# A hybrid encoder layer on one core: branch mix by row block with its weights loaded once, six PSUM banks for the mix, and three projection weight slots ahead of LayerNorm 1

## The chip, the cores and the metric

The kernel runs on one NeuronCore of a Trainium2 chip. A core has a matrix engine (TensorE, PE in the profile), a vector engine (VectorE, DVE), a scalar engine (ScalarE, ACT), GpSimd (POOL) and SyncE (SP), which issues the DMAs here. Each engine works through its own queue in order and waits for the others by semaphores. The metric is the time of one execution in device microseconds; a kernel's time is the median of its runs.

## What is computed

One layer with post-norm residuals, for two request groups (BATCH 1 and DEC_BATCH 1, 512 tokens each, D_MODEL 1024) that share all weights:

```python
x = layernorm(ALPHA * x + 0.5 * swiglu(x, ffn1_wgu, ffn1_wd))          # FFN1, LN1
h = x @ w_in                                                           # MLA, RWKV and gate columns
br_a = mla(h) @ p_mla                                                  # attention branch
br_b = rwkv7(h) @ p_rwkv                                               # recurrent branch, 512 channels
gates = sigmoid(h[..., OFF_GATE:] + b_gate).reshape(b, s, 2, D_MODEL)
mix = (gates[:, :, 0] * br_a + gates[:, :, 1] * br_b) @ w_o            # the branch mix, then w_o
x = layernorm(ALPHA * x + mix)                                         # LN2
x = layernorm(ALPHA * x + cross(x, layernorm(mem)))                    # LN3
x = layernorm(ALPHA * x + 0.5 * swiglu(x, ffn2_wgu, ffn2_wd))          # FFN2, LN4
```

Everything is float32.

## The kernel before

**Layout.** Activations lie with channels on the 128 partitions and the 512 tokens of one group along the row: D_MODEL is eight such tiles (KT), a group one of two (G). Operands are of the type fp32r in the profile: each float32 operand is split into a high and a low part, and a product of a 128 x 128 weight block with a 128 x 512 tile is three matmuls: high by high, high by low, low by high (`Bank.prod`). A `Bank` is one PSUM bank; the ring "a" has four, "b" and "c" two each. `abreast(banks, ws, xs)` computes several rows of an output at once, going over the inner tiles in the outer loop, so that each tile of x serves all rows as soon as it is there. In the profile the parts are called by their tiles: `xh`/`xl` are the high and low parts of x, `yh`/`yl` of the recurrence's output, `mh`/`ml` of the mix, `whl` both parts of a weight slot, `ps` a bank.

**Weights.** Apart from the feed-forward parts, weights come as a stream of 512 KB slots of eight blocks each, in the order of a plan. `Stream.fetch` takes the next one: SP loads it into a raw buffer (`wraw`), ACT casts it to the high part (L246), DVE subtracts to get the low part (L180). There are two raw buffers; the split slots go round rings of buffers (pools `wp` with three and `wide` with one, later `wp` and `wb_pool`). `st.block()` hands out the blocks and fetches the next slot when one is used up.

**Order.** A scheduler sets the order of the instructions on each engine from the order in which the code issues them, its own costs and the dependencies. Two places force it: `Bank` keeps the matmuls of one bank in order, and the DVE engine handed to the kernel (`Held`) puts every instruction issued after `BlockNorm.stats(..., hold=True)` behind the statistics of that layer norm. That includes the subtractions of `Stream.fetch`.

**FFN1 and LN1.** FFN1 multiplies by Strassen's seven products in blocks; its last step, `down_step` for the last entry of DOWN, adds the last sums into x. The sums' products go in a list of eight orders, and before each one `ahead(i)` is called, which fetches weights. LN1 then takes its statistics through transposes on PE (`cc`, `ln_v`, `ln_h` and `x` in PE's L221 rows; `ln_b`, `ln_m`, `rs` on DVE), and a chain on DVE, ACT and POOL normalises and splits x. The first use of x is `compressed`, three rows of w_in (one slot a row) by both groups abreast: 144 matmuls, called c_kv below.

**The recurrence and what runs beside it.** The RWKV recurrence goes head by head (four pairs of heads); each step is a chain of small matmuls (`sn`, `gs`, `uv`) and DVE operations, and matmuls of other parts fill PE's time between them. Its output y is 4 tiles a group; the last tile (the fourth head pair) crosses PE in L216 and L221 rows `ps<-cc,z` (`crossed`) before it can be split to `yh` and `yl`.

**The branch mix.** For group 0 and then group 1, eight rows n: four weight blocks of p_rwkv (half a slot), the gate `gt` and the attention branch `at` by DMA, twelve matmuls into a bank of ring "a", and z = (gt + 1) * sum, z = z + at, split to `mh` and `ml` on ACT and DVE (three DVE operations). The plan lists the four p_rwkv slots twice (`B_MIX` = slots 12 to 16 of stream B), so they are loaded and split once for each group. Of the matmuls, those on the first three tiles of y of the first rows can go before the last head pair is ready: 36 stand ahead of the crossing in PE's order. Then w_o follows, rows 0 to 3 and 4 to 7, each by both groups, one row after the other (`mix_row`), with 24 matmuls a row and its sum added to x for LN2.

Of the kernel before, what the change touches and what calls it, by code (L numbers as in the profile page):

```python
# [22 lines left out]
G = 2  # L23
D = 1024
KT = 8
# [7 lines left out]
ALPHA = 2.0**0.25  # L33
# [25 lines left out]
A_FILL = A_END - 16  # L59

FILL = ((72, 66, 30), (6, 50, 36), (8, 54, 36), (0, 38, 20))
B_MIX = 12, 16
STREAM_B = (
    tiles_of("w_ck", range(4), 8)
    + [("w_cv", k, n) for k in range(8) for n in range(4)]
# [461 lines left out]
            ra, rb = nxt  # L527


def ffn(k, fw, x32, std, rows_of, op_tile, posts, sums, d_h, d_s, norm_of, applied, last=False):  # L530

# [31 lines left out]
    norms, due, going = [], [], []  # L565
# [18 lines left out]
    def down_step(n, u2, u4):  # L584
        m, p0, p1_ = DOWN[n]

        def ahead(i):

            if i == 2 and m == 3:
                while due:  # L590
                    due.pop(0)()
            if i == 2:
                for p in range(p1_, max([p1_, *(b for _, _, b in DOWN[n + 1 : n + 2])])):
                    fetch(p)
# [3 lines left out]

        def add(out, name, u):
            nc.vector.scalar_tensor_tensor(out=out, in0=ps[name].t, scalar=SC, in1=u, op0=ALU.mult, op1=ALU.add)  # L600

        final = n == len(DOWN) - 1

        def more(r, c, u):

# [8 lines left out]
        def summed(i, x):  # L614

            x.add(m // 2)
            if m == 3 and not last:
                if i == 1:  # L620
                    going.append(applied(rows_of[0], norms[0]))
                    for _ in range(3):
                        next(going[0])
                BlockNorm.stats([x], True)
            elif m == 3 and i == 1:
                BlockNorm.stats(norms, True)
# [25 lines left out]
    with posts() as sb:  # L652
# [13 lines left out]
        for g in range(G):  # L666
            xp = [std[g].pair(i) for i in range(KT)]
            banks = [Bank(k, "a") for _ in range(4)]
            ws = [[(o[0][:, i * P : i * P + P], o[1][:, i * P : i * P + P]) for i in range(KT)] for o in w]
            if last:  # L670
                abreast(banks, ws, xp)
            for j in range(2):
                pg, pu = banks[2 * j : 2 * j + 2]
                if not last:
                    for b, o in zip((pg, pu), ws[2 * j : 2 * j + 2]):
                        b.prod(b.t, list(zip(o, xp)))
                s = sb.tile([P, 2, T], F32, name="s", tag="s", bufs=2)[:, 0]
                nc.scalar.activation(out=s, in_=pg.t, func=AF.Silu)
                nc.vector.tensor_tensor(out=s, in0=s, in1=pu.t, op=ALU.mult)
                to_h(s, d_s[j][g], sb)  # L680
            if g == 0:
                for name in ("S1", "S2", "S3"):
                    ops[name] = op_tile(name)
                hold = [(0, slice(0, 2), sb.tile([P, 2, T], F32, name="up", tag="up", bufs=1))]
                for i in range(2):
                    t = sb.tile([P, 1, T], F32, name=("p1", "u4")[i], tag=("p1", "u4")[i], bufs=1)
                    hold.append((2, slice(i, i + 1), t))
                for name, a, b, op in (("S1", "A21", "A22", ALU.add), ("S2", None, "A11", ALU.subtract)):
                    for h in hold:
                        sums_of(name, a, b, op, *h)  # L690
# [7 lines left out]
        for f in range(2 * NP):  # L698
# [41 lines left out]
            if f % 2:  # L740
# [13 lines left out]
                a, b = hs  # L754
# [48 lines left out]
def kernel(  # L803
# [87 lines left out]
    xpools = [x0.enter_context(pool("x0", "right")), rs.enter_context(pool("x1", "right"))]  # L891
    wide = rs.enter_context(pool("ww", "right"))
    plan = [(wa, 0, A_FILL)] + [(wa, A_FILL, A_END)] * G
    plan += [(wb, 0, B_MIX[1]), (wb, *B_MIX), (wb, B_MIX[1], len(STREAM_B) // 8)]
    st = Stream(nc, plan, nc.vector)
    st.use(*[(wp, 3, 2)] * 3, (wide, 1, 0))
    k.ps = ctx.enter_context(pool("banks", space=PSUM))
    with ExitStack() as f1:
# [35 lines left out]

        places = {n: (xpools[0], "x", 4) for n in ("A11", "A12")}
        places.update({n: (xpools[1], "x", 4) for n in ("A22", "S4")}, **{n: (xo, "xo", 6) for n in ("S1", "S2", "S3")})
        ffn(k, fw, x32, xs, (0, 1), op_tiles(places), lambda: pool("post1"), sums1, d_h, d_s, norm1, applied1)

    def gate_out(n, g, h, t):
        nc.scalar.activation(out=t, in_=h, func=AF.Tanh, scale=0.5, bias=hbg[:, n : n + 1])  # L940
# [334 lines left out]
    def acts(kts, name):  # L1275
        return Acts(mixed, "xs", 8, kts, name)

    mix = []
    with pool("mixin", "right") as sm:
        for g in range(G):  # L1280
            mix.append(acts(KT, "m"))
            for n in range(KT):
                w = st.blocks(4)
                gt = sm.tile([P, T], F32, name="gt", tag="gt", bufs=6)
                at = sm.tile([P, T], F32, name="at", tag="at", bufs=6)
                nc.sync.dma_start(out=gt, in_=d_gate[8 + n][:, g])
                nc.sync.dma_start(out=at, in_=d_a[n][:, g])
                b = Bank(k, "a")
                b.prod(b.t, list(zip(w, [ys[g].pair(i) for i in range(4)])))
                z = sm.tile([P, T], F32, name="z", tag="z", bufs=3)  # L1290
                nc.vector.scalar_tensor_tensor(out=z, in0=gt, scalar=1.0, in1=b.t, op0=ALU.add, op1=ALU.mult)
# [30 lines left out]
    norms = norms_of(2)  # L1322
    w = []

    def mix_row(g, n):
        b = Bank(k, "a")
        b.prod(b.t, list(zip(w[n], [mix[g].pair(i) for i in range(KT)])))
        sum_row(norms[g], g, n, b, 0.5 / ALPHA)

    for n0 in (0, 4):  # L1330
        w += [st.blocks(KT) for _ in range(4)]
        for g in range(G):
            for n in range(n0, n0 + 4):
                mix_row(g, n)
            if (n0, g) == (4, 0):
                norms[0].stats()
    x2 = [None, None]
# [115 lines left out]

    places = {n: (mixed, "xs", 8) for n in ("A11", "A12", "A22", "S4")}
    places.update({n: (keep, "xs", 4) for n in ("S1", "S2")}, S3=(of, "xo", 2))
    ffn(k, fw, y32, x3, (1, 0), op_tiles(places), lambda: pool("post2"), sums2, d_h, d_s, norm4, applied4, True)


def softmax(k, sb, s, scale):
# [544 lines left out]
```

## Time and profile before

| | us |
|---|---|
| time, median of 3 runs (lowest to highest) | 2775.86 (2774.26 to 2776.49) |
| the profiled execution | 2775.84 |
| its span, first to last instruction | 2774.1 |
| mean granted PE clock (share of full speed) | 0.963 |
| PE busy / DVE busy | 2605.6 / 2123.8 |
| last transposes of LN1 to the first full run of c_kv matmuls | 684.45 to 700.71 |
| last crossing of the recurrence to the first w_o matmul | 1773.98 to 1822.64 |

A profile's row reads: start and length in microseconds, engine, line of kernel.py, operation, the tile written and the tiles read, the shapes, how many instructions the row gathers, and in brackets how long the engine was idle before it and which engine's result ended that. L216 and L221 are the helper lines through which all matmuls and transposes go, L180 the one for DVE, L246 the cast to the high part, so a row is told by its tiles. PE rows can overlap, since matmuls are pipelined; the distance between starts is what one costs.

### The profile page before, as it was taken

What the parts mean: (1) busy time and instruction counts of PE and PEld (TensorE: products, weight loads), DVE (VectorE), ACT (ScalarE), POOL (GpSimd) and SP (SyncE); (2) the same over time, 40 slices, a digit from 0 to 9 for tenths busy, and PEclk for the clock granted to TensorE, in tenths of its full rate; (3) what the DMA queues carried; (4) which work ended last, traced back from release to release, by engine and by line L of the source; (5) the groups of instructions that cost most, each with busy time, mean ns of one, the idle gap of its engine ahead of it and who ended that gap; (6) DMA issues with size and microseconds to landing.
All of it is one profiled execution on the core that took longest, in us unless ns stands there. A gap on an engine that the chain in (4) does not pass through costs nothing.

```text
span 2774.1 us, 41500 instructions
## 1 busy us (share of the span) xinstructions
PE 2605.6 (94%) x15600; PEld 2079.9 (75%) x15600; DVE 2123.8 (77%) x3749; ACT 1095.9 (40%) x2008; POOL 699.1 (25%) x479
## 2 busy tenths in 40 slices
PE   8999999997899999997989888899999999999996
PEld 7888887785767777776777676677777888887784
DVE  7888887999366777758475768656798888887987
ACT  5334342223353555444443432224554343342222
POOL 0323332443100001133133321103032332332443
PEclk9999999999989999998899898999999999999998
DMA  4344437661244333343434354441101433447751
GB/s 171 130 150 160 152 145 296 235 235 57 95 165 150 112 106 111 111 143 129 131 109 131 119 178 126 161 174 42 54 31 67 161 144 138 152 162 267 273 202 68
DMA packets 164776, 398.18 MB, mean 144 GB/s; under 512 B 41120, under 2 KB 47520, under 8 KB 164576
## 3 DMA queue, kind: packets, MB, share of 16 engines
q1 hardware_dynamic: 164576, 395.53, 40.8%
q8 instruction: 124, 2.03, 0.3%
q14 instruction: 76, 0.62, 0.1%
HBM read 261.50 MB, written 133.96 MB: 143 GB/s over the span
## 4 chain that ended last, share of the span: by engine, by line
PE 76%; DVE 15%; ACT 3%; issue 2%; DMA 2%; POOL 1%; SPq 0%; POOLq 0%; ACTq 0%; DVEq 0%
PE ps L216 73%; PE ps L221 3%; DVE whl L180 2%; DVE dw L180 2%; DVE z L180 1%; DVE x L180 1%; DVE tm L180 1%; DVE rs L180 1%; DVE wt L180 1%; DVE s L180 1%; DVE ln_s L180 1%; DVE phi L180 1%; ACT whl L246 0%; DMA ld<-d_rw 0%; DVE up L180 0%
## 5 line engine op out<-in xcount | busy, mean ns | idle before, releaser
L216 PE MATMUL ps<-xh,whl 128*128 128x512 f32 x2688 | 890.2, 402 | 26.7 <-DVE whl L180 16.8
L216 PE MATMUL ps<-xo,whl 128*128 128x512 f32 x3792 | 899.7, 396 | 14.2 <-DVE z L180 8.5
L216 PEld LDWEIGHTS ps<-xo,whl 128*128 128x128 f32 x3792 | 713.0, 189 | 185.6 <-DVE z L180 6.7
L216 PEld LDWEIGHTS ps<-xh,whl 128*128 128x128 f32 x2688 | 507.8, 190 | 144.2 <-DVE whl L180 20.4
L216 PE MATMUL ps<-xl,whl 128*128 128x512 f32 x1344 | 535.1, 399 | 1.5 <-POOL xl L247 1.5
L180 DVE TENSOR_TENSOR whl<-wraw,whl 128x512 fp32r<-128x512 f32 (+4 forms) x273 | 282.5, 1045 | 63.6 <-ACT whl L246 62.9
L246 ACT CAST whl<-wraw 128x512 fp32r<-128x512 f32 (+4 forms) x318 | 223.9, 715 | 250.1 <-PE ps L216 210.8
L216 PEld LDWEIGHTS ps<-xl,whl 128*128 128x128 f32 x1344 | 255.8, 190 | 55.8 <-POOL xl L247 2.3
L709 POOL TENSOR_TENSOR s<-s,up 128x512 f32<-128x512 f32 x80 | 115.9, 1449 | 626.6 <-DVE up L180 391.1
L246 ACT CAST whl<-wt 128x512 fp32r<-128x512 f32 (+3 forms) x280 | 148.5, 555 | 276.0 <-PE ps L216 164.1
L180 DVE TENSOR_TENSOR whl<-wt,whl 128x512 fp32r<-128x512 f32 (+3 forms) x280 | 216.7, 795 | 10.8 <-ACT whl L246 10.3
L247 POOL TENSOR_TENSOR whl<-wraw,whl 128x1024 fp32r<-128x1024 f32 x45 | 109.1, 2426 | 385.5 <-ACT whl L246 355.4
L246 ACT CAST hop<-s 128x512 fp32r<-128x512 f32 x128 | 79.5, 621 | 238.2 <-POOL s L709 178.0
L180 DVE TENSOR_TENSOR hop<-s,hop 128x512 fp32r<-128x512 f32 x128 | 121.4, 949 | 55.4 <-ACT hop L246 48.0
L180 DVE SCALAR_TENSOR_TENSOR x<-ps,x 128x512 f32<-128x512 f32 x184 | 124.5, 683 | 50.6 <-PE ps L216 50.2
L180 DVE TENSOR_TENSOR wt<-wraw 128x512 f32<-128x512 f32 (+3 forms) x140 | 110.6, 791 | 1.0
L180 DVE TENSOR_TENSOR wt<-wraw,wt 128x512 f32<-128x512 f32 (+3 forms) x140 | 103.1, 737 | 4.2 <-DMA wraw<-in_wf_dram 2.1
L607 POOL TENSOR_TENSOR x<-x,s 128x512 f32<-128x512 f32 x48 | 70.7, 1478 | 129.4 <-DVE x L180 129.4
L247 POOL TENSOR_TENSOR xl<-x,xh 128x512 fp32r<-128x512 f32 x48 | 68.6, 1453 | 91.8 <-ACT xh L246 91.5
L180 DVE TENSOR_TENSOR p<-ps,p 128x512 f32<-128x512 f32 x120 | 82.2, 685 | 7.8 <-PE ps L216 4.8
L607 POOL TENSOR_TENSOR x<-x,z 128x512 f32<-128x512 f32 x48 | 71.3, 1486 | 52.8 <-DVE x L180 49.2
L216 PE MATMUL ps<-mh,whl 128*128 128x512 f32 x256 | 82.2, 401 | 0.0
(328 smaller groups left out, 3728.2 us busy)
## 6 DMA issues: line engine op xcount, KB each, us to landing
d_h<-hop SPq DMA_DIRECT2D x140, 512.0 KB, 2.6
xo<-d_h SPq DMA_DIRECT2D x140, 512.0 KB, 7.2
wraw<-in_wf_dram SPq DMA_DIRECT2D x95, 512.0 KB, 3.4
wraw<-in_wa_dram SPq DMA_DIRECT2D x57, 512.0 KB, 3.5
wraw<-in_wb_dram SPq DMA_DIRECT2D x36, 512.0 KB, 3.4
wraw<-in_wf_dram SPq DMA_DIRECT2D x36, 384.0 KB, 3.9
ld<-d_rw SPq DMA_DIRECT2D x24, 512.0 KB, 4.7
d_gate<-t SPq DMA_DIRECT2D x32, 256.0 KB, 2.4
```

Of the source, the lines that this page charges most:

```text
L180: inst = f(*args, **kw)
L216: self.last = order(k.tc, k.nc.tensor.matmul(out, a, b, start=start, stop=stop), self.last)
L221: self.last = order(self.k.tc, self.k.nc.tensor.transpose(out, a, ident), self.last)
L246: nc.scalar.copy(hi, src)
L247: (low or nc.vector).tensor_tensor(out=lo, in0=src, in1=hi.bitcast(F32), op=ALU.subtract)
L607: eng.tensor_tensor(out=y[r, c], in0=y[r, c], in1=u, op=ALU.add)
L709: nc.gpsimd.tensor_tensor(out=s[:, i], in0=s[:, i], in1=up[:, i], op=ALU.mult)
```

## The change

1. The branch mix goes over rows n outside and groups inside, so each half slot of p_rwkv serves both groups, and the four slots are loaded and split once. The plan no longer lists them twice.
2. The sums of the mix go to six banks, "aaaabb" in turn, instead of four.
3. w_o's first four rows of group 0 go abreast; all other rows as before.
4. The last down step of FFN1 calls `early()` at its fifth product, which fetches the first three slots of w_in. `ffn`'s flag `last` is replaced by the presence of `early`.

```diff
--- before.py
+++ after.py
@@ -59,7 +59,6 @@
 A_FILL = A_END - 16
 
 FILL = ((72, 66, 30), (6, 50, 36), (8, 54, 36), (0, 38, 20))
-B_MIX = 12, 16
 STREAM_B = (
     tiles_of("w_ck", range(4), 8)
     + [("w_cv", k, n) for k in range(8) for n in range(4)]
@@ -527,7 +526,9 @@
             ra, rb = nxt
 
 
-def ffn(k, fw, x32, std, rows_of, op_tile, posts, sums, d_h, d_s, norm_of, applied, last=False):
+def ffn(k, fw, x32, std, rows_of, op_tile, posts, sums, d_h, d_s, norm_of, applied, early=None):
...
@@ -584,11 +585,15 @@
     def down_step(n, u2, u4):
         m, p0, p1_ = DOWN[n]
 
+        final = n == len(DOWN) - 1
+
         def ahead(i):
 
             if i == 2 and m == 3:
                 while due:
                     due.pop(0)()
+            if i == 4 and final and early:
+                early()
             if i == 2:
                 for p in range(p1_, max([p1_, *(b for _, _, b in DOWN[n + 1 : n + 2])])):
                     fetch(p)
@@ -598,8 +603,6 @@
 
         def add(out, name, u):
             nc.vector.scalar_tensor_tensor(out=out, in0=ps[name].t, scalar=SC, in1=u, op0=ALU.mult, op1=ALU.add)
-
-        final = n == len(DOWN) - 1
 
         def more(r, c, u):
 
@@ -616,7 +619,7 @@
 
 
             x.add(m // 2)
-            if m == 3 and not last:
+            if m == 3 and early:
                 if i == 1:
                     going.append(applied(rows_of[0], norms[0]))
                     for _ in range(3):
@@ -667,11 +670,11 @@
             xp = [std[g].pair(i) for i in range(KT)]
             banks = [Bank(k, "a") for _ in range(4)]
             ws = [[(o[0][:, i * P : i * P + P], o[1][:, i * P : i * P + P]) for i in range(KT)] for o in w]
-            if last:
+            if not early:
                 abreast(banks, ws, xp)
             for j in range(2):
                 pg, pu = banks[2 * j : 2 * j + 2]
-                if not last:
+                if early:
                     for b, o in zip((pg, pu), ws[2 * j : 2 * j + 2]):
                         b.prod(b.t, list(zip(o, xp)))
                 s = sb.tile([P, 2, T], F32, name="s", tag="s", bufs=2)[:, 0]
@@ -891,7 +894,7 @@
     xpools = [x0.enter_context(pool("x0", "right")), rs.enter_context(pool("x1", "right"))]
     wide = rs.enter_context(pool("ww", "right"))
     plan = [(wa, 0, A_FILL)] + [(wa, A_FILL, A_END)] * G
-    plan += [(wb, 0, B_MIX[1]), (wb, *B_MIX), (wb, B_MIX[1], len(STREAM_B) // 8)]
+    plan += [(wb, 0, len(STREAM_B) // 8)]
     st = Stream(nc, plan, nc.vector)
     st.use(*[(wp, 3, 2)] * 3, (wide, 1, 0))
     k.ps = ctx.enter_context(pool("banks", space=PSUM))
@@ -934,7 +937,8 @@
 
         places = {n: (xpools[0], "x", 4) for n in ("A11", "A12")}
         places.update({n: (xpools[1], "x", 4) for n in ("A22", "S4")}, **{n: (xo, "xo", 6) for n in ("S1", "S2", "S3")})
-        ffn(k, fw, x32, xs, (0, 1), op_tiles(places), lambda: pool("post1"), sums1, d_h, d_s, norm1, applied1)
+        ffn(k, fw, x32, xs, (0, 1), op_tiles(places), lambda: pool("post1"), sums1, d_h, d_s, norm1, applied1,
+            lambda: [st.fetch() for _ in range(3)])
 
     def gate_out(n, g, h, t):
         nc.scalar.activation(out=t, in_=h, func=AF.Tanh, scale=0.5, bias=hbg[:, n : n + 1])
@@ -1275,17 +1279,17 @@
     def acts(kts, name):
         return Acts(mixed, "xs", 8, kts, name)
 
-    mix = []
+    mix = [acts(KT, "m") for _ in range(G)]
     with pool("mixin", "right") as sm:
-        for g in range(G):
-            mix.append(acts(KT, "m"))
-            for n in range(KT):
-                w = st.blocks(4)
+        for n in range(KT):
+            w = st.blocks(4)
+            for g in range(G):
                 gt = sm.tile([P, T], F32, name="gt", tag="gt", bufs=6)
                 at = sm.tile([P, T], F32, name="at", tag="at", bufs=6)
                 nc.sync.dma_start(out=gt, in_=d_gate[8 + n][:, g])
                 nc.sync.dma_start(out=at, in_=d_a[n][:, g])
-                b = Bank(k, "a")
+
+                b = Bank(k, "aaaabb"[(2 * n + g) % 6])
                 b.prod(b.t, list(zip(w, [ys[g].pair(i) for i in range(4)])))
                 z = sm.tile([P, T], F32, name="z", tag="z", bufs=3)
                 nc.vector.scalar_tensor_tensor(out=z, in0=gt, scalar=1.0, in1=b.t, op0=ALU.add, op1=ALU.mult)
@@ -1322,16 +1326,19 @@
     norms = norms_of(2)
     w = []
 
-    def mix_row(g, n):
-        b = Bank(k, "a")
-        b.prod(b.t, list(zip(w[n], [mix[g].pair(i) for i in range(KT)])))
-        sum_row(norms[g], g, n, b, 0.5 / ALPHA)
+    def mix_rows(g, ns):
+        banks = [Bank(k, "a") for _ in ns]
+        if (g, ns[0]) == (0, 0):
+            abreast(banks, w, [mix[g].pair(i) for i in range(KT)])
+        for n, b in zip(ns, banks):
+            if (g, ns[0]) != (0, 0):
+                b.prod(b.t, list(zip(w[n], [mix[g].pair(i) for i in range(KT)])))
+            sum_row(norms[g], g, n, b, 0.5 / ALPHA)
 
     for n0 in (0, 4):
         w += [st.blocks(KT) for _ in range(4)]
         for g in range(G):
-            for n in range(n0, n0 + 4):
-                mix_row(g, n)
+            mix_rows(g, range(n0, n0 + 4))
             if (n0, g) == (4, 0):
                 norms[0].stats()
     x2 = [None, None]
@@ -1453,7 +1460,7 @@
 
     places = {n: (mixed, "xs", 8) for n in ("A11", "A12", "A22", "S4")}
     places.update({n: (keep, "xs", 4) for n in ("S1", "S2")}, S3=(of, "xo", 2))
-    ffn(k, fw, y32, x3, (1, 0), op_tiles(places), lambda: pool("post2"), sums2, d_h, d_s, norm4, applied4, True)
+    ffn(k, fw, y32, x3, (1, 0), op_tiles(places), lambda: pool("post2"), sums2, d_h, d_s, norm4, applied4)
 
 
 def softmax(k, sb, s, scale):
```

The changed file has one line less ahead of the helpers, so its L179, L215, L220 and L245 are the L180, L216, L221 and L246 of the profile.

DVE at the end of LN1, before: the low parts of the slots (`whl<-wraw,whl`) and the operations of LN1's scaling ahead of them.

```order
L180 TENSOR_TENSOR z<-x_211,ps 128x512
L180 TENSOR_TENSOR s<-s,ps 128x512
L180 TENSOR_TENSOR z<-z,ps 128x512
L180 TENSOR_TENSOR s<-x_211,ps 128x512
L180 TENSOR_TENSOR whl<-wraw,whl 128x1024
L180 TENSOR_TENSOR s<-s,ps 128x512
L180 TENSOR_TENSOR whl<-wraw,whl 128x1024 x3
```

After: among LN1's statistics (`BN_STATS`), the first two slots.

```order
L179 SCALAR_TENSOR_TENSOR z<-ps,z 128x512
L179 BN_STATS ln_b<-ps 128x6 x2
L179 TENSOR_TENSOR whl<-wraw,whl 128x1024
L179 BN_STATS ln_b<-ps 128x6 x3
L179 SCALAR_TENSOR_TENSOR s<-ps,z 128x512
L179 TENSOR_TENSOR whl<-wraw,whl 128x1024
L179 TENSOR_TENSOR x_211<-x_211,s 128x512 x2
L179 SCALAR_TENSOR_TENSOR x_211<-ps,x_211 128x512
L179 BN_STATS ln_b<-ps 128x6 x2
L179 BN_AGGR ln_m<-ln_b 128x2 x2
L179 BN_STATS ln_b<-ps 128x6 x2
L179 BN_AGGR ln_m<-ln_b 128x2 x2
```

The two subtractions moved from the last DVE operations of LN1's scaling to before the first aggregate of its statistics; the third slot's stands some 15 rows further down, between two of FFN1's last sums, and of the x3 before one is left near the end of LN1.

PE at the end of the recurrence, before: `yh_16288` and `yl_16289` are the parts of y of group 0, `cc,z` the crossings of the last head pair.

```order
L216 MATMUL ps<-yl_16289,whl 128x512
L216 MATMUL ps<-yh_16288,whl 128x512
L216 MATMUL ps<-cc,z 64x64 x8
L221 MATMUL ps<-cc,z 64x64 x8
L216 MATMUL ps<-cc,z 64x64 x8
L221 MATMUL ps<-cc,z 64x64 x8
L216 MATMUL ps<-yh_16288,whl 128x512
L216 MATMUL ps<-yl_16289,whl 128x512
L216 MATMUL ps<-yh_16288,whl 128x512 x2
```

After: `yh_16302` and `yl_16303` are those of group 1.

```order
L215 MATMUL ps<-yh_16302,whl 128x512
L215 MATMUL ps<-yl_16303,whl 128x512
L215 MATMUL ps<-yh_16302,whl 128x512 x2
L215 MATMUL ps<-yl_16303,whl 128x512
L215 MATMUL ps<-yh_16302,whl 128x512 x2
L215 MATMUL ps<-yl_16303,whl 128x512
L215 MATMUL ps<-yh_16302,whl 128x512
L215 MATMUL ps<-cc,z 64x64 x8
L220 MATMUL ps<-cc,z 64x64 x8
L215 MATMUL ps<-cc,z 64x64 x8
L220 MATMUL ps<-cc,z 64x64 x8
L215 MATMUL ps<-yh_16288,whl 128x512 x3
```

Ahead of the crossings there now stand matmuls of both groups, 54 instead of 36.

SP in the mix, before: loads of the gate (`gt`), of branch A (`at`) and of weight slots.

```order
L1286 DMA gt<-d_gate_68 128x512
L1287 DMA at<-d_a_130 128x512
L142 DMA wraw<-in_wb_dram 128x1024
L1286 DMA gt<-d_gate_69 128x512
L1287 DMA at<-d_a_131 128x512
L1286 DMA gt<-d_gate_70 128x512
L1287 DMA at<-d_a_132 128x512
L142 DMA wraw<-in_wb_dram 128x1024
L1286 DMA gt<-d_gate_71 128x512
L1287 DMA at<-d_a_133 128x512
```

After: the end of the loads of the mix, and the start of LN2's loads of x.

```order
L1290 DMA at<-d_a_135 128x512
L1289 DMA gt<-d_gate_74 128x512
L1290 DMA at<-d_a_136 128x512
L1289 DMA gt<-d_gate_74 128x512
L1290 DMA at<-d_a_136 128x512
L141 DMA wraw<-in_wb_dram 128x1024 x4
L1317 DMA x_16872<-d_x_0_57 128x1024
L1317 DMA x_16872<-d_x_1_58 128x1024
```

The weight loads that stood between those of the gate and branch A are gone or have moved behind the last of these 32 loads. One slot, w_o's first, moved the other way: its load now stands ahead of all 32.

## The prediction

> **What bounds the kernel now.** I read the page's busy times first, then the chain that ended last, then a table of busy time by stretch, then the rows of the places that the change touches. The page's lines say that TensorE (PE) is the bound almost everywhere: 94% busy, and matmuls carry 76% of the chain.
>
> ```profile
> PE 2605.6 (94%) x15600; PEld 2079.9 (75%) x15600; DVE 2123.8 (77%) x3749; ACT 1095.9 (40%) x2008; POOL 699.1 (25%) x479
> ...
> PE 76%; DVE 15%; ACT 3%; issue 2%; DMA 2%; POOL 1%; SPq 0%; POOLq 0%; ACTq 0%; DVEq 0%
> ```
>
> The change removes no matmul, so it can only pay where PE waits or runs at a low clock. Busy time by stretch (window, length, busy us of each engine with its instructions, the granted PE clock as a share, DMA share, GB/s):
>
> ```profile
> core 0: us, PE busy (x) PEld busy (x) DVE busy (x) ACT busy (x) POOL busy (x), PEclk, DMA share, GB/s
> 640.00:700.00 60.00, 33.91 (x177) 26.45 (x175) 56.93 (x110) 23.37 (x36) 23.89 (x18) 0.84 0.17 67
> 700.00:735.00 35.00, 33.61 (x137) 26.58 (x138) 9.38 (x10) 9.85 (x16) 7.15 (x6) 0.94 0.31 105
> ...
> 1755.00:1780.00 25.00, 18.29 (x204) 14.28 (x204) 18.43 (x51) 4.25 (x9) 3.05 (x3) 0.85 0.42 141
> 1780.00:1823.00 43.00, 40.47 (x158) 32.40 (x159) 34.90 (x52) 15.57 (x23) 0.00 (x0) 0.89 0.58 195
> 1823.00:1920.00 97.00, 96.43 (x419) 77.60 (x418) 54.72 (x81) 30.75 (x44) 21.21 (x15) 0.98 0.26 93
> 2059.00:2092.00 33.00, 29.19 (x112) 22.20 (x111) 32.53 (x52) 19.60 (x30) 18.92 (x12) 0.79 0.20 64
> ```
>
> PE is idle 26 of 60 us at the end of LayerNorm 1 (LN1), while DVE is busy 57 of the 60. Around the branch mix it loses some 9 us and runs at a clock of 0.85 to 0.89. w_o right behind it has no gap. The last row is the start of the second feed-forward part (FFN2), with a clock of 0.79.
>
> **LN1: three weight slots fetched early.** The timeline of PE, then of ACT, DVE, POOL and SP:
>
> ```profile
> 684.45 1.09 PE L221 MATMUL ps<-cc,ln_v 128*128 128x128 f32 x4 [5.70 <-DVE ln_v L180]
> 685.33 1.06 PE L221 MATMUL ps<-cc,ln_h 128*128 128x128 f32 x4
> 700.71 1.22 PE L216 MATMUL ps<-xh,whl 128*128 128x512 f32 x2 [14.32 <-DVE whl L180]
> ```
> ```profile
> 652.82 1.04 ACT L246 CAST whl<-wraw 128x1024 fp32r<-128x1024 f32 x1
> 661.82 1.05 ACT L246 CAST whl<-wraw 128x1024 fp32r<-128x1024 f32 x1 [7.96 <-PE ps L216]
> 674.92 0.81 ACT L359 ACTIVATE x<-z,vc 128x512 f32<-128x512 f32 x1 [12.04 <-DVE z L180]
> ...
> 704.63 1.05 ACT L246 CAST whl<-wraw 128x1024 fp32r<-128x1024 f32 x1 [1.81 <-DMA wraw<-in_wa_dram]
> ...
> 734.52 0.59 ACT L1002 COPY c<-ps 128x512 f32<-128x512 f32 x1 [10.59 <-PE ps L216]
> ```
> ```profile
> 661.78 0.69 DVE L180 SCALAR_TENSOR_TENSOR s<-ps,z 128x512 f32<-128x512 f32 x1 [0.71 <-PE ps L216]
> ...
> 664.52 0.69 DVE L180 SCALAR_TENSOR_TENSOR x<-ps,x 128x512 f32<-128x512 f32 x1 [0.72 <-PE ps L216]
> ...
> 699.37 1.29 DVE L180 TENSOR_TENSOR whl<-wraw,whl 128x1024 fp32r<-128x1024 f32 x1
> ...
> 701.18 1.70 DVE L180 TENSOR_TENSOR whl<-wraw,whl 128x1024 fp32r<-128x1024 f32 x1
> ...
> 705.72 1.88 DVE L180 TENSOR_TENSOR whl<-wraw,whl 128x1024 fp32r<-128x1024 f32 x1 [2.84 <-ACT whl L246]
> ```
> ```profile
> 676.46 1.27 POOL L247 TENSOR_TENSOR xl<-x,xh 128x512 fp32r<-128x512 f32 x1 [23.11 <-ACT xh L246]
> ...
> 688.43 18.08 POOL L247 TENSOR_TENSOR xl<-x,xh 128x512 fp32r<-128x512 f32 x13 [5.72 <-ACT xh L246]
> ```
> ```profile
> 700.68 0.33 SPq L142 DMA_DIRECT2D wraw<-in_wa_dram  x1
> ```
>
> The high halves of the first two slots were made at 652.82 and 661.82, but their low halves only at 699.37 and 701.18, because these subtractions stood behind all of LN1 on DVE. So c_kv (144 matmuls, three rows by two groups, one slot a row) had 4 matmuls done and sent 140 from 700.71. In the changed order the low halves stand among LN1's statistics, two ahead of the first aggregate and one right behind the first spread's numbers, and 18 c_kv matmuls precede LN1's last spread (the x4 and x4 at 684.45).
>
> What it adds: three low halves on DVE within LN1. An undisturbed one takes 1.22 us (1803.01, shown below), so 3.7 us. The two idle gaps at 661.78 and 664.52 take 1.4 of that; the rest, 2.2 us, delays LN1's chain and moves the spread's end from 686.39 to 688.6. On SP the third slot's DMA now stands ahead of the stores of x, and its ACT cast ahead of LN1's scaling: issued when the first raw buffer comes free (about 660), its landing by the old row's 3.95 us (700.68 to 704.63) is 664, before the first scaling at 674.92, so I cost it at nothing. If that cover is gone, ACT holds the scaling, and with it PE.
>
> From 688.6 there are 126 matmuls. Cold ones take 0.44 us and warm ones 0.227 (both worked out below). With 13 cold, as after the stall at 1804.29: 13 x 0.44 + 113 x 0.227 = 31.4, end at 720.0. The same form for before: 700.71 + 13 x 0.44 + 127 x 0.227 = 735.2, against ACT's copy of the second group's first row at 734.52. Gain **15.2**. POOL's low halves of x come every 18.08 / 13 = 1.39 us, and each feeds 9 matmuls (2.05 us), so POOL does not take over.
>
> Bounds: low halves at 1.88 us (705.72, POOL at work) and no early matmul beyond the 4 give 15.2 - 2.0 - 3.2 = 10; no delay of LN1 and a warm clock give 15.2 + 2.2 + 2.8 = 20. I take 15.2, nearest to undisturbed rows, since POOL was idle for 23.11 us before 676.46. [...]
>
> **The mix.** PE's timeline, then the split of one slot on DVE, ACT and SP:
>
> ```profile
> 1744.81 1.14 PE L216 MATMUL ps<-cc,z 64*64 64x64 f32 x16
> ...
> 1748.08 0.97 PE L216 MATMUL ps<-sn,ar 64*64 64x64 f32 x32
> ...
> 1764.76 0.68 PE L216 MATMUL ps<-uv,phi 128*64 128x64 f32 x14
> ...
> 1768.68 0.39 PE L216 MATMUL ps<-yh,whl 128*128 128x512 f32 x1
> 1773.98 1.94 PE L216 MATMUL ps<-cc,z 64*64 64x64 f32 x16 [4.92 <-DVE z L180]
> ...
> 1779.72 0.79 PE L216 MATMUL ps<-yh,whl 128*128 128x512 f32 x1
> ...
> 1783.83 0.62 PE L216 MATMUL ps<-yh,whl 128*128 128x512 f32 x2
> ...
> 1789.27 0.62 PE L216 MATMUL ps<-yh,whl 128*128 128x512 f32 x2
> ...
> 1801.05 0.50 PE L216 MATMUL ps<-yh,whl 128*128 128x512 f32 x1 [0.48 <-ACT whl L246]
> ...
> 1804.29 1.22 PE L216 MATMUL ps<-yh,whl 128*128 128x512 f32 x2 [2.05 <-DVE whl L180]
> ...
> 1810.00 0.75 PE L216 MATMUL ps<-yh,whl 128*128 128x512 f32 x2
> ...
> 1822.64 0.40 PE L216 MATMUL ps<-mh,whl 128*128 128x512 f32 x1
> ```
> ```profile
> 1803.01 1.22 DVE L180 TENSOR_TENSOR whl<-wraw,whl 128x1024 fp32r<-128x1024 f32 x1
> ```
> ```profile
> 1799.95 1.04 ACT L246 CAST whl<-wraw 128x1024 fp32r<-128x1024 f32 x1
> ```
> ```profile
> 1793.28 0.38 SPq L142 DMA_DIRECT2D wraw<-in_wb_dram  x1
> ```
>
> Warm: 24 matmuls from 1783.83 to 1789.27, 0.227 each. Cold: 13 from 1804.29 to 1810.00, 0.44 each. The parts:
> - 18 more matmuls (54 for 36) fit into the 4.92 us before the last crossing, which waits for DVE's z: 18 x 0.227 = 4.1.
> - The crossings took 1773.98 to 1779.72 = 5.74 us cold; the same work between 1744.81 and 1748.08 took 3.27 warm: 2.5.
> - The 11 matmuls from 1779.72 to 1783.83 took 4.11, warm 2.5: 1.6.
> - The second pass over the weights goes, and with it the stalls of 0.48 and 2.05 us (the slot issued at 1793.28 was split at 1799.95 and 1803.01): 2.5; and the cold run behind them, 13 x 0.21 = 2.8. Its four DMAs, four casts and four subtractions were otherwise hidden.
>
> Sum 13.4; w_o could start at 1809.2. DVE was busy 34.9 of the 43 us from 1780 to 1823, which left PE free of it. Without the four subtractions of the second pass (4 x 1.22) it has 30.0 us to do, and PE's share ends in 1809.2 - 1777.3 (the crossings' end, 1773.98 + 3.27) = 31.9. So DVE just keeps up, and is nearly full: whatever it must do more, w_o's first subtractions above all, comes late.
>
> What comes late next is w_o. Its first four rows run abreast and need all four slots soon, where before it needed one. One slot waits loaded but is split only when the last p_rwkv outputs of group 0 leave its memory; the others' DMAs stand on SP behind all 32 loads of gate and branch A. PE's first four or five matmuls need only what is there; then the second slot's low half (some 1.05 of cast and 1.22 of subtraction after the end of the mix, less what overlaps) holds it about 2 us, which DVE's load makes no shorter. A slow clock behind it costs 2.8 or nothing; half is 1.4. Bounds: no wait, 13.4; one whole chain of DMA, cast and subtraction (3.95 + 1.05 + 1.22 = 6.2) plus 2.8 cold leaves 4.4. I take 13.4 - 3.4 = **10.0**, nearer to the end with the shorter chain, since one slot is loaded and two raw buffers take the next.
>
> The row at 1804.29 is cold after an idle time of 2.05 us. [...]
>
> **FFN2's start.** The slots' ring is left in another phase, and the order has one of the first FFN2 splits earlier. The window has 3.8 us of PE idle time and a low clock; between 0 (covered by LayerNorm 3) and 5, I take **1.5**: most of the idle time there waits for FFN2's own splits, but only one of them moves. Everything else keeps its order.
>
> Sum 15.2 + 10.0 + 1.5 = 26.7. The profiled execution took 2775.84 (span 2774.1 and 1.7 around it), practically the median, 2775.86; so 2749.1, say **2749**.
>
> **Rivals.**
> - *w_o starves for a chain* (mix 4.4): total 21.1, 2755. For it speaks SP's order; against, two raw buffers and 15 matmuls for the first two slots ahead of the third.
> - *LN1's chain suffers*: the third cast waits for a buffer or for its DMA on ACT and holds the scaling. LN1 then brings 8 (the wait until the scaling's own cover is gone, 7 us), total 19.5, 2756. Against: ACT's casts all lie before 675.
> - *The banks don't help*: the two other banks still hold recurrence sums, so the 18 matmuls don't run early, and the crossing stays cold: 4.1 + 2.5 + 1.6 = 8.2 less, total 18.5, 2757. Against: the last matmuls of the recurrence begin at 1764.76, and in PE's order the 18 stand behind them.
> - *FFN2 gets all of its 5 and w_o doesn't wait*: 15.2 + 13.4 + 5 = 33.6, 2742.
> - *Slower*: w_o's four slots come strictly one after another behind the mix, 4 x 6.2 = 25 us, with 96 matmuls in short cold bursts, 96 x 0.21 = 20. That takes 45 from 15.2 + 13.4 + 1.5 = 30.1: 15 slower, 2791. It decides once waits and cold there exceed 35 us. Against: the first two slots load before the mix ends.
>
> **How the numbers follow.** Forecast 0.57 (own range 2744 to 2754), w_o chain 0.13, LN1 0.10, banks 0.05, more than forecast 0.10, slower 0.03, two failures that leave under 5.6 us (0.2%, about what this kernel's measurement can tell) 0.02. So faster 0.95, same 0.02, slower 0.03. The range 2740 to 2760 takes in all the faster cases with some slack for their sizes.
>
> **What would show it.** Right: the low halves of the first slots near 660 and 663 and no idle time of 14 us before c_kv; ACT's copy of the second group's first row near 719; no idle time of 4.9 us before the last crossing, which takes 3.3; the first mh matmul 13 us nearer to the crossing. Wrong: scaling on ACT waiting for a cast; w_o's first matmuls waiting over 3 us for DVE whl; c_kv starting after 690.

## The result and the profile after

The changed kernel takes 2747.2 us (median of 4 runs, 2740.56 to 2751.1) against 2776.18 for the kernel before (4 runs): 29 us less, a ratio of 0.9895 with an interval of 0.9873 to 0.9916. The forecast was 2749 in 2740 to 2760. The profiled execution has a span of 2747.4, 26.7 below that of before.

The busy line of the page, then busy time by stretch as before (640 to 700 and 2037 to 2070 stand for the same places as the rows shown ahead; 1744 to 1768 is the end of the recurrence with the crossing):

```profile
PE 2597.5 (95%) x15600; PEld 2074.1 (75%) x15600; DVE 2118.7 (77%) x3745; ACT 1090.2 (40%) x2004; POOL 699.2 (25%) x479
```
```profile
core 0: us, PE busy (x) PEld busy (x) DVE busy (x) ACT busy (x) POOL busy (x), PEclk, DMA share, GB/s
640.00:700.00 60.00, 50.97 (x236) 40.05 (x235) 56.80 (x108) 21.82 (x33) 19.95 (x16) 0.91 0.23 80
...
1744.00:1768.00 24.00, 22.55 (x233) 17.39 (x234) 18.17 (x53) 4.66 (x9) 2.69 (x3) 1.00 0.44 147
1768.00:1812.00 44.00, 42.73 (x187) 34.60 (x186) 35.84 (x54) 15.78 (x22) 0.00 (x0) 1.00 0.67 232
...
2037.00:2070.00 33.00, 28.47 (x131) 21.94 (x130) 32.66 (x54) 21.33 (x33) 18.84 (x12) 1.00 0.20 64
```

DVE has four operations fewer (3749 to 3745, the second pass over p_rwkv) and PE as many as before. PE now does 236 matmuls in the 60 us at LN1's end instead of 177, and the clock in the mix and at FFN2's start is 1.00, where it was 0.85 to 0.89 and 0.79.

**LN1.** PE, DVE, ACT and POOL of the changed kernel:

```profile
681.95 0.78 PE L215 MATMUL ps<-xh,whl 128*128 128x512 f32 x1
...
689.62 0.62 PE L220 MATMUL ps<-cc,ln_v 128*128 128x128 f32 x4 [1.18 <-DVE ln_v L179]
690.07 0.60 PE L220 MATMUL ps<-cc,ln_h 128*128 128x128 f32 x4
...
693.57 0.96 PE L215 MATMUL ps<-xh,whl 128*128 128x512 f32 x3 [1.04 <-ACT xh L245]
```
```profile
661.18 1.20 DVE L179 TENSOR_TENSOR whl<-wraw,whl 128x1024 fp32r<-128x1024 f32 x1
...
665.33 1.23 DVE L179 TENSOR_TENSOR whl<-wraw,whl 128x1024 fp32r<-128x1024 f32 x1
...
675.78 1.22 DVE L179 TENSOR_TENSOR whl<-wraw,whl 128x1024 fp32r<-128x1024 f32 x1
...
704.53 5.29 DVE L179 TENSOR_TENSOR whl<-wraw,whl 128x1024 fp32r<-128x1024 f32 x1
```
```profile
671.64 1.05 ACT L245 CAST whl<-wraw 128x1024 fp32r<-128x1024 f32 x1 [6.35 <-PE ps L215]
...
679.42 0.81 ACT L358 ACTIVATE x<-z,vc 128x512 f32<-128x512 f32 x1 [4.03 <-DVE z L179]
...
724.42 0.59 ACT L1006 COPY c<-ps 128x512 f32<-128x512 f32 x1 [4.90 <-PE ps L215]
```
```profile
693.60 15.14 POOL L246 TENSOR_TENSOR xl<-x,xh 128x512 fp32r<-128x512 f32 x12 [5.72 <-ACT xh L245]
712.05 1.27 POOL L246 TENSOR_TENSOR xl<-x,xh 128x512 fp32r<-128x512 f32 x1 [3.32 <-ACT xh L245]
```

The three low halves stand where the order put them and last 1.2 us each. c_kv begins at 681.95, ahead of the last spread at 689.62, and no wait of 14 us is left. One row was not foreseen: the fourth slot's low half at 704.53, the one left near LN1's end, lasts 5.29 us, while POOL makes one low half of x after the other; the last part of x then comes late (712.05, after a wait of 3.32 for ACT), and PE waits for it too:

```profile
712.03 0.99 PE L215 MATMUL ps<-xh,whl 128*128 128x512 f32 x2 [2.49 <-ACT xh L245]
```

**The mix.** PE of the changed kernel:

```profile
1761.99 0.39 PE L215 MATMUL ps<-yh,whl 128*128 128x512 f32 x1
1762.47 1.14 PE L215 MATMUL ps<-cc,z 64*64 64x64 f32 x16
...
1765.17 0.63 PE L220 MATMUL ps<-cc,z 64*64 64x64 f32 x8
...
1798.74 0.50 PE L215 MATMUL ps<-mh,whl 128*128 128x512 f32 x1 [1.27 <-ACT whl L245]
```

The early matmuls end as z comes, the crossing takes 3.3 us, and the first w_o matmul is 36.3 us behind the crossing's start (48.7 before). It waits 1.27 us for ACT, at a clock that stays at 1.00. The cast that it waits for ends at 1798.68 and was itself held until PE's last p_rwkv matmul ended at 1797.48:

```profile
1797.64 1.04 ACT L245 CAST whl<-wraw 128x1024 fp32r<-128x1024 f32 x1 [1.96 <-PE ps L215]
```

Between landmarks that both kernels have, the length of each stage can be compared whatever lies ahead of it. The landmarks are the end of FFN1's last gap of 3.0 us on PE (before at 644.58, after at 647.07), ACT's first copy of c of group 1, the start of the last crossing, the first mh matmul, FFN2's first xh matmul (before at 2059.15, after at 2037.17) and the span's end. All kernels of the experiments stand in the table (us, one profiled execution each):

| kernel | gap to c | c to crossing | crossing to w_o | w_o to FFN2 | FFN2 to end |
|---|---|---|---|---|---|
| before | 89.9 | 1039.5 | 48.7 | 236.5 | 715.0 |
| changed | 77.4 | 1038.1 | 36.3 | 238.4 | 710.2 |
| changed, again | 73.6 | 1042.6 | 36.3 | 235.4 | 709.6 |
| mix only | 90.9 | 1041.7 | 36.3 | 239.7 | 710.3 |
| early slots only | 73.7 | 1041.0 | 45.8 | 236.1 | 714.8 |
| fourth low half on POOL | 74.8 | 1038.3 | 36.3 | 239.7 | 710.3 |
| four banks | 73.7 | 1037.7 | 44.0 | 237.4 | 710.2 |
| row by row | 73.1 | 1043.2 | 36.3 | 239.6 | 710.3 |
| ring phase of before | 76.6 | 1044.6 | 34.8 | 236.2 | 715.3 |
| four early slots | 74.9 | 1039.7 | 36.3 | 235.5 | 710.2 |
| four early, ring of before for w_o | 74.0 | 1041.8 | 34.9 | 242.1 | 710.3 |

From before to changed: 12.6 us less, 1.4 less, 12.4 less, 1.9 more, 4.7 less; with 2.5 more ahead of FFN1's last gap that makes 26.7. The second and fourth columns differ between kernels with the same code there, the second by up to 6.5 us (1038.1 to 1044.6), the fourth by 4.3 (235.4 to 239.7). The other three repeat within 1 us, but for causes named below.

### The profile page after: what moved, and what is told of

It reads as the page before. It is cut to its first block, busy times and chain, and to the rows that moved or that the text cites. A ratio compares the mean times of both kernels' runs of the same rounds, so it can differ in the third digit from the quotient of the medians.

```text
span 2747.4 us, 41481 instructions
## 1 busy us (share of the span) xinstructions
PE 2597.5 (95%) x15600; PEld 2074.1 (75%) x15600; DVE 2118.7 (77%) x3745; ACT 1090.2 (40%) x2004; POOL 699.2 (25%) x479
## 4 chain that ended last, share of the span: by engine, by line
PE 54%; DVE 11%; issue 3%; ACT 3%; DMA 2%; POOL 1%; SPq 0%; POOLq 0%; ACTq 0%; DVEq 0%
PE ps L215 51%; PE ps L220 3%; DVE whl L179 1%; DVE dw L179 1%; DVE x L179 1%; DVE z L179 1%; DVE rs L179 1%; DVE phi L179 1%; DVE tm L179 1%; DVE ln_s L179 1%; DMA ld<-d_rw 1%; DVE wt L179 0%; ACT whl L245 0%; DMA d_q<-st 0%; POOL ln_z L357 0%
## 5 line engine op out<-in xcount | busy, mean ns | idle before, releaser
L215 PE MATMUL ps<-xo,whl 128*128 128x512 f32 x3792 | 899.3, 396 | 14.1 <-DVE z L179 8.5
L215 PE MATMUL ps<-xh,whl 128*128 128x512 f32 x2688 | 889.3, 402 | 15.7 <-ACT xh L245 11.4
L215 PEld LDWEIGHTS ps<-xo,whl 128*128 128x128 f32 x3792 | 712.9, 189 | 185.7 <-DVE z L179 6.7
L215 PEld LDWEIGHTS ps<-xh,whl 128*128 128x128 f32 x2688 | 508.1, 190 | 132.0 <-ACT xh L245 13.0
L215 PE MATMUL ps<-xl,whl 128*128 128x512 f32 x1344 | 536.5, 399 | 1.4 <-POOL xl L246 1.4
L179 DVE TENSOR_TENSOR whl<-wraw,whl 128x512 fp32r<-128x512 f32 (+4 forms) x269 | 280.4, 1052 | 53.2 <-ACT whl L245 52.7
L245 ACT CAST whl<-wraw 128x512 fp32r<-128x512 f32 (+4 forms) x314 | 219.7, 711 | 247.2 <-PE ps L215 226.4
L215 PEld LDWEIGHTS ps<-xl,whl 128*128 128x128 f32 x1344 | 255.9, 190 | 56.4 <-POOL xl L246 2.7
L245 ACT CAST whl<-wt 128x512 fp32r<-128x512 f32 (+3 forms) x280 | 148.5, 555 | 272.5 <-PE ps L215 160.7
L179 DVE TENSOR_TENSOR whl<-wt,whl 128x512 fp32r<-128x512 f32 (+3 forms) x280 | 215.5, 791 | 11.5 <-ACT whl L245 11.4
L246 POOL TENSOR_TENSOR whl<-wraw,whl 128x1024 fp32r<-128x1024 f32 x45 | 109.4, 2433 | 385.8 <-ACT whl L245 353.3
L245 ACT CAST hop<-s 128x512 fp32r<-128x512 f32 x128 | 79.5, 621 | 246.1 <-POOL s L712 180.3
L179 DVE TENSOR_TENSOR hop<-s,hop 128x512 fp32r<-128x512 f32 x128 | 121.4, 949 | 58.3 <-ACT hop L245 50.7
L179 DVE SCALAR_TENSOR_TENSOR x<-ps,x 128x512 f32<-128x512 f32 x184 | 124.5, 683 | 53.6 <-PE ps L215 53.0
L179 DVE TENSOR_TENSOR wt<-wraw 128x512 f32<-128x512 f32 (+3 forms) x140 | 109.9, 785 | 1.0
L179 DVE TENSOR_TENSOR wt<-wraw,wt 128x512 f32<-128x512 f32 (+3 forms) x140 | 102.8, 734 | 4.6 <-DMA wraw<-in_wf_dram 2.6
L246 POOL TENSOR_TENSOR xl<-x,xh 128x512 fp32r<-128x512 f32 x48 | 66.8, 1420 | 98.2 <-ACT xh L245 97.9
L179 DVE TENSOR_TENSOR p<-ps,p 128x512 f32<-128x512 f32 x120 | 82.2, 685 | 7.2 <-PE ps L215 4.0
L215 PE MATMUL ps<-mh,whl 128*128 128x512 f32 x256 | 81.1, 397 | 1.3 <-ACT whl L245 1.3
```

The costliest lines, as they stand in the source:

```text
L179: inst = f(*args, **kw)
L215: self.last = order(k.tc, k.nc.tensor.matmul(out, a, b, start=start, stop=stop), self.last)
L245: nc.scalar.copy(hi, src)
L246: (low or nc.vector).tensor_tensor(out=lo, in0=src, in1=hi.bitcast(F32), op=ALU.subtract)
```

## The experiments

The first four ran on one chip beside the kernel before (2776.33, 11 runs), the next four likewise (2778.26, 9 runs), and the last (2778.19, 8 runs).

**The changed kernel again**

> The changed kernel once more, unchanged, to see its own spread. In its first profile PE reached the end of FFN1 2.5 us later than in the kernel before (last gap of FFN1 at 647.07 against 644.58), although nothing is changed there: the first 40 us held 122 matmuls against 133. Theory: this is chance at the start of an execution, so the gap at FFN1's end will lie anywhere between 644 and 648 in another profile, and the distances between later stages stay as they were (spread's end to the second group's first copy of c some 34 us; last crossing 3.3 us; clock 1.00 at FFN2's start). Rival: the changed kernel's start differs for a reason of its own, and 647 comes again. Time by both: 2742 to 2750.

2747.4 us (2747.15 to 2748.57), ratio 0.9896 (0.988 to 0.9913). FFN1's last gap came at 647.89, so by the letter the rival's 647 came again. It settles little: in the other kernels with the same three early slots it lay between 645.0 (row by row) and 647.2 (early slots only), so it varies by some 3 us without a cause in the code. What did not repeat is the fourth low half:

```profile
705.24 1.51 DVE L179 TENSOR_TENSOR whl<-wraw,whl 128x1024 fp32r<-128x1024 f32 x1
```
```profile
694.30 17.34 POOL L246 TENSOR_TENSOR xl<-x,xh 128x512 fp32r<-128x512 f32 x13 [5.72 <-ACT xh L245]
```
```profile
721.49 0.59 ACT L1006 COPY c<-ps 128x512 f32<-128x512 f32 x1 [4.85 <-PE ps L215]
```

With 1.51 instead of 5.29 us there, POOL's 13 operations stay together and the stage from the gap to c takes 73.6 us instead of 77.4. So LN1 brings 16.3 us in one case and 12.6 in the other. Of the six profiles with three early slots and this subtraction on DVE, four have the short case (1.51 or 1.52 us) and two the long one (5.29).

**Mix only**

```diff
-            lambda: [st.fetch() for _ in range(3)])
+            lambda: None)
```

> The changed kernel without the early fetch of the three slots (mix by row block, six banks, w_o abreast stay). Theory: the parts add up, LN1's end is as in the kernel before (14 us of PE idle time before c_kv), the mix brings its 12 us, and the start of FFN2 its 4 to 5, since those come from the other phase of the slot ring: about 16 us below the kernel before, 2760. Rival: FFN2's gain comes only from PE's state or from the earlier shift and goes with the early fetch: 12 us below, 2764.

2761.3 us (2759.82 to 2765.43), ratio 0.9947 (0.9935 to 0.996): 15 below before. The theory's parts are there: LN1 as before (90.9), the mix at 36.3, and FFN2 at 710.3, which needs no early slots.

**Early slots only** (mix, plan and w_o of the kernel before, `early` kept)

> The kernel before with only the early fetch of the three slots; mix, banks, plan and w_o are those of before. Theory: LN1 brings about 12.5 us, the mix and FFN2's start are as in the kernel before (waits of 4.9, 0.5 and 2.1 us, clock near 0.8 at FFN2): 2763.5. Rival: FFN2's start also gains 4 to 5: 2759.

2759.47 us (2757.65 to 2761.18), ratio 0.9938 (0.9926 to 0.9951): 17 below, 4 better than the theory, but not by the rival, since FFN2 takes 714.8. LN1 gave 16.2 where 12.5 was expected (the fourth low half lasted 1.52), and the mix is 2.9 shorter although it was not touched. PE's timeline there:

```profile
1761.95 1.94 PE L216 MATMUL ps<-cc,z 64*64 64x64 f32 x16 [4.93 <-DVE z L180]
...
1792.18 0.73 PE L216 MATMUL ps<-yh,whl 128*128 128x512 f32 x2 [1.98 <-DVE whl L180]
```

This is the stall of 2.05 us at 1804.29 before, at 1.98; but two matmuls behind it take 0.73 us, not 1.22. The clock was kept this time: 1.00 from 1789 to 1800, where before shows 0.50 from 1804.29 to 1810.00. So the 2.8 us that the prediction put on that cold run can go without the mix being touched; with one profile of each kernel, how often that happens is not known.

**The fourth low half on POOL**

```diff
-        split(nc, hl[:, 0], hl[:, 1], raw, self.low)
+        split(nc, hl[:, 0], hl[:, 1], raw, nc.gpsimd if self.n == 3 else self.low)
```

> The changed kernel, but the low half of the fourth slot is subtracted on POOL instead of DVE; nothing else. In the changed kernel's profile this subtraction took 5.29 us on DVE (1.2 elsewhere) while POOL made the low halves of x one after the other, and the last part of x came 4 us late. Theory: the two engines held each other up, and PE then waited for the last x (2.5 and 1.0 us, on ACT's xh): without it DVE's last operation of LN1 ends 5 us earlier and c_kv's second group 3 to 4 us earlier, 2744 with the other kernel at 2747. Rival: PE had other work in the meantime and catches up, so c_kv ends within 1 us of where it did: no difference. Second rival: POOL's own subtraction (2.4 us by the other rows of POOL) delays the first low half of x, and c_kv starts 2 us later.

2751.05 us (2746.43 to 2752.63), ratio 0.9905 (0.989 to 0.9921): not faster. The end of LN1 is rid of the long subtraction (from the gap to c 74.8 us, 2.6 less than with the 5.29 us), but POOL did the subtraction earlier, for 2.37 us, and a DVE operation begun beside it lasted until it ended. POOL and DVE of this kernel:

```profile
670.95 2.37 POOL L246 TENSOR_TENSOR whl<-wraw,whl 128x1024 fp32r<-128x1024 f32 x1 [17.48 <-ACT whl L245]
```
```profile
671.10 2.24 DVE L179 SCALAR_TENSOR_TENSOR rs<-rs,ln_v 128x4 f32<-128x4 f32 x1
673.38 0.16 DVE L179 SCALAR_TENSOR_TENSOR rs<-rs 128x4 f32<-128x4 f32 x1
```

An operation on 128x4 elements, 0.16 us in the row behind it, lasts 2.24 us, to 673.34; POOL's subtraction, begun 0.15 us ahead of it, ends at 673.32. It sits in LN1's chain, so the first spread came 2.1 us later after the gap (29.54 us instead of 27.45). The second rival was right in kind: the delay is on DVE's chain, not on POOL's first low half of x. The two operations end within 0.02 us of each other; why they do is not shown.

**Four banks**

```diff
-                b = Bank(k, "aaaabb"[(2 * n + g) % 6])
+                b = Bank(k, "a")
```

> The changed kernel with the mix's sums in the four banks of ring a, as before, instead of six; row blocks, weights once, abreast and early slots stay. Theory: the two other banks are what lets 54 instead of 36 matmuls go ahead of the crossing; with four, 36 go ahead, PE waits 4.9 us at the crossing and runs it at the low clock (5.7 instead of 3.3), so from the crossing's start to the first w_o matmul pass 4.1 + 2.5 + some 1.5 more than the 36.3 us of the changed kernel: 44 to 45, and the time is 7 to 8 us higher, 2755. Rival: the order by row block is what matters and the banks only shift the wait: under 3 us more, 2750.

2751.6 us (2750.94 to 2757.2), ratio 0.9913 (0.99 to 0.9927). From the crossing to w_o 44.0 us, 7.7 more than with six banks, as the theory said; 36 matmuls stand ahead of the crossing again, and the wait (4.25 us) and the cold crossing (5.7 us instead of 3.3) are back:

```profile
1757.93 1.94 PE L215 MATMUL ps<-cc,z 64*64 64x64 f32 x16 [4.25 <-DVE z L179]
...
1801.93 0.50 PE L215 MATMUL ps<-mh,whl 128*128 128x512 f32 x1 [1.27 <-ACT whl L245]
```

So of the mix's 12.4 us the two further banks carry 7.7. The rest is 4.7 against the profile of before, and 1.8 against early slots only, whose profile kept its clock behind the stall. It is left to the order by row block with its weights loaded once, by which the stalls of 0.48 and 2.05 us go and the wait of 1.27 us comes; no run separates these.

**Row by row**

```diff
-        if (g, ns[0]) == (0, 0):
+        if False:
             abreast(banks, w, [mix[g].pair(i) for i in range(KT)])
         for n, b in zip(ns, banks):
-            if (g, ns[0]) != (0, 0):
+            if True:
```

> The changed kernel with w_o's first four rows of group 0 one after the other again instead of abreast. Theory: the last part of the mix comes late on DVE (its last ml began at 1802.39, w_o at 1798.74), and the first row needs all eight parts of the mix for its 24 matmuls, of which the last 3 can't go before about 1803; 21 matmuls last 4.8 us, so PE waits about 1 us there and the second slot is no longer needed at once, which saves nothing else: 0 to 2 us slower, 2747 to 2749. Rival: the four slots abreast cost the 1.27 us wait that PE has at w_o's start, and row by row is faster by 1 us.

2748.14 us (2746.52 to 2749.48), ratio 0.9895 (0.988 to 0.991). Crossing to w_o is 36.3 with the same wait of 1.27, and w_o to FFN2 239.6, within what that column does by itself. Four rows abreast neither cost nor bring anything that shows; the theory and the rival both priced an effect that doesn't show. PE's first row waits as before, so the wait is for the first slot alone.

**The ring's phase of before**

```diff
-    st.use((wp, 3, 2), (wb_pool, 2, 0), (wp, 3, 2), (wb_pool, 2, 0), (wp, 3, 2))
+    st.use((wp, 3, 2), (wp, 3, 2), (wb_pool, 2, 0), (wp, 3, 2), (wb_pool, 2, 0))
```

> The changed kernel, with the list of buffer rings for the slots from w_o on turned by one place, so that every slot of w_o, w_cq and w_co gets the buffer that it had in the kernel before (four slots fewer ahead of it turn the phase). Theory: FFN2's 4.7 us come from that phase alone, so from FFN2's first matmul to the end it takes 714.8 again instead of 710.2; the wait at w_o's start (1.27 us for a buffer that group 0's y leaves late) goes, since w_o's first slot gets a free buffer: 4.6 - 1.3 = 3.3 us slower, 2750.5. Rival: FFN2's start is better because the order of its weights changed with the stream's length, whatever the ring: 1.3 us faster, 2746.

2745.83 us (2743.37 to 2754.89), ratio 0.9895 (0.9879 to 0.9911). The time as a whole doesn't show the 3.3 us that were expected, and the profiled execution was the slowest of the five (2754.89). Its stages say what was expected: FFN2 to end 715.3 as in the kernel before, and w_o without its wait, 34.8. PE at w_o, then at FFN2's start:

```profile
1801.54 0.40 PE L215 MATMUL ps<-mh,whl 128*128 128x512 f32 x1
```
```profile
2039.63 0.50 PE L215 MATMUL ps<-xh,whl 128*128 128x512 f32 x1 [0.78 <-ACT whl L245]
...
2044.93 2.00 PE L215 MATMUL ps<-xh,whl 128*128 128x512 f32 x3 [2.25 <-DVE whl L179]
...
2048.44 1.22 PE L215 MATMUL ps<-xh,whl 128*128 128x512 f32 x2 [0.65 <-DVE whl L179]
```

In the changed kernel the largest wait for DVE whl in that stretch is 0.32 us:

```profile
2047.89 0.73 PE L215 MATMUL ps<-xh,whl 128*128 128x512 f32 x2 [0.32 <-DVE whl L179]
```

So the four slots fewer turn the ring, and the stalls with the low clock behind them (0.84 here from 2037 to 2070, 1.00 in the changed kernel) go: 4.7 us, by luck of the count. All three profiles with the old phase take 714.8 to 715.3 in this stage, all eight with the new one 709.6 to 710.3. That the first weights find a free buffer earlier is the reading of it; no run shows the buffers themselves. The 5.29 us at LN1's end came again in this profile; DVE's row:

```profile
702.43 5.29 DVE L179 TENSOR_TENSOR whl<-wraw,whl 128x1024 fp32r<-128x1024 f32 x1
```

**Four early slots**

```diff
-            lambda: [st.fetch() for _ in range(3)])
+            lambda: [st.fetch() for _ in range(4)])
```

> The changed kernel with four slots fetched early instead of three, so that the fourth low half stands on DVE among LN1's statistics and not beside POOL's low halves of x near its end. Theory: in the three-slot version that subtraction takes 1.5 or 5.3 us by chance (POOL's work at the same time); among the statistics it takes 1.2 but delays LN1's spread by as much, so the distance from FFN1's last gap to c_kv's second group is 73.6 to 75 in every execution: no gain against the fast case of three slots, 2747, and 2 to 4 less against its slow case. Rival: the cast of the fourth slot waits for its buffer and holds ACT's scaling in LN1: over 3 us slower.

2744.21 us (2741.12 to 2746.33), ratio 0.9881 (0.9868 to 0.9895). The third and the fourth low half now both stand in LN1's first chain, one of them at a place that is new, and take 1.22 us each:

```profile
670.94 1.22 DVE L179 TENSOR_TENSOR whl<-wraw,whl 128x1024 fp32r<-128x1024 f32 x1
...
674.33 1.22 DVE L179 TENSOR_TENSOR whl<-wraw,whl 128x1024 fp32r<-128x1024 f32 x1
```

Gap to c is 74.9, between the two cases of three slots, as the theory said. The median is the lowest of all, but its interval overlaps that of the changed kernel.

**Four early slots and the ring turned for w_o alone**

```diff
+    st.use((wp, 3, 2), (wb_pool, 2, 0), (wp, 3, 2), (wb_pool, 2, 0), (wp, 3, 2))
     x2 = [None, None]
```

(with the four early slots and the turned list ahead of w_o, as in the diffs of the two runs above; those lines are left out here)

> The changed kernel with four early slots, and with the ring turned back by one place for the eight slots of w_o alone, so that w_o's first slot gets a free buffer and FFN2 keeps the phase of the changed kernel. Theory (the parts are independent): from FFN1's last gap to c_kv's second group 74.9 us, from the crossing to the first w_o matmul 34.8 instead of 36.3, from FFN2's first matmul to the end 710.2; that is 1.4 us below the version with four early slots: 2743, with 2747 for the changed kernel. Rival: FFN2's start depends on w_o's buffers too, and it takes 714.8: 2747.5.

2745.62 us (2744.65 to 2751.75), ratio 0.9885 (0.9869 to 0.9901). The three stages came as forecast (74.0, 34.9, 710.3), so the theory stands for the stages and the rival falls; but w_o to FFN2 took 242.1 in the profiled execution, the longest of all. That stretch in the changed kernel's second profile, then here:

```profile
1800.40:2035.79 235.39, 226.36 (x1096) 182.53 (x1097) 165.59 (x369) 105.12 (x218) 46.52 (x34) 0.99 0.20 65
```
```profile
1797.70:2039.75 242.05, 232.89 (x1097) 187.30 (x1096) 167.16 (x372) 105.97 (x219) 47.24 (x34) 0.96 0.19 62
```

PE's idle time is nearly the same (9.0 and 9.2 us); it is busy 6.5 us longer, at a clock of 0.96 instead of 0.99. The ring-phase kernel, whose w_o has the same buffers, took 236.2. So w_o's buffers alone don't make the stretch long; why the clock was lower stays open. No version was shown to beat the changed kernel by more than its scatter.

## Why the prediction was right

**LN1, 15.2 forecast.** It brought 16.3 where the fourth low half took 1.5 us and 12.6 where it took 5.3. Its steps held: the spread was delayed by 1.8 us where 2.2 were forecast (690.67 for its end, against 686.39 before, less 2.5 that were lost ahead of FFN1's gap), and c_kv started ahead of it. The third cast on ACT did wait, until 671.64 and for PE, where the prediction had only its DMA, until 664; but it came 7.8 us ahead of the first scaling (679.42) and held nothing. What was missed is the slot left behind: the prediction weighed the longer times with POOL at work (1.88 us) for the three moved halves, which took 1.20 to 1.23, and not for the fourth, whose place it had in the order. That fourth subtraction alone moves LN1's gain by 3.7 us.

**The mix, 10.0 forecast.** It brought 12.4 against the profile of before and 9.5 against the execution that kept its clock behind the stall (45.8 to 36.3). The step that was mis-sized is the wait at w_o: 2 us for the second slot's low half and 1.4 for the clock were put down, and 1.27 for the first slot's high half came, with a clock of 1.00 behind it (1798.74 to 1804.00). The first slot was late, not the second: its cast begins only when the last p_rwkv matmul has ended (1797.64 behind 1797.48), a wait that the prediction saw and then passed over. With the ring turned so that this slot has a free buffer, the wait is gone. The prices of the early matmuls, the crossing and the matmuls behind it add up to 8.2 there, and the four banks gave back 7.7.

**FFN2, 1.5 forecast.** It brought 4.7, close to the upper bound of 5. The mechanism, the ring's other phase, is the one that the ring-phase run bears out; the size was off by a factor of three. The prediction took a low value because only one split moves in the order; with that one moved, the waits for ACT and DVE of 0.78, 2.25 and 0.65 us that the old phase has shrink to one of 0.32.

**The sum.** 26.7 was forecast and 26.7 is the difference of the spans, but the agreement of the single profile is partly chance: 2.5 us lost at the start, and LN1's slow case, stand against FFN2's larger gain. The medians differ by 29.

**The rivals.** The banks' price was right and the rival false; w_o's chain and the slower rival did not come: PE waits there once, 1.27 us. LN1's chain was not held by the third cast. The rival with FFN2's full 5 came near for FFN2 (4.7), but w_o did wait.

## What to carry to other kernels

Where an order forces work behind a long chain on an engine, look not only at what moves out but also at what is left, and at the other engines' stream that it then meets. A change in the number of slots turns every ring behind it: look at which later stage starts on a free buffer. When single times scatter by as much as the parts that are in question, compare the lengths between landmarks that both kernels have.

## What was not expected of the hardware

- A subtraction on DVE that takes 1.2 us while POOL is idle met a stream of POOL subtractions of 1.26 us each (16.36 for 13). In the kernel before it took 1.29, 1.70 and 1.88 us there; at its place in the changed kernel it took 1.51 or 1.52 in four profiles and 5.29 in two. Begun at 704.53, it ended only after POOL's stream had paused at 708.74, past three changes from one POOL operation to the next (704.9, 706.2 and 707.5, an estimate from 1.26 us each behind 693.60). Begun at 705.24, it ended at 706.75, 1.1 us behind the first change (705.6, by the same estimate behind 694.30), and POOL's 13 operations took 17.34 us instead of the 16.36 that they take with this subtraction on POOL. It started 10.9 us behind the start of POOL's stream in both, so what decides between the two isn't seen.
- Behind an idle time of PE of 2 us the clock was low for 13 matmuls in one execution and full in another (0.50 from 1804.29 to 1810.00 behind 2.05 us, 1.00 from 1789 to 1800 around 1.98 us). Stages with the same code vary by 4 to 7 us between executions, more than most terms of the sum. From w_o to FFN2 it is the clock: PE's idle time is 9.0, 8.9 and 9.2 us in the changed kernel's second profile, its first and the last version, while the granted clock is 0.99, 0.98 and 0.96 and the stretch 235.4, 238.4 and 242.1 us long.
